# Attention projections with low parts of their weights from adding transfers, and the depthwise convolution moved forward, in a hybrid encoder layer

## The chip, the core and the metric

One core of a Trainium2 chip runs the whole program. The metric is the device time of one execution in microseconds (us). Five engines matter: TensorE (PE) for matrix products, VectorE (DVE), ScalarE (ACT) and GpSimd (POOL) for everything elementwise, and SyncE (SP), which issues most of the transfers from memory. Each engine works through its own instructions strictly in the order in which they stand in its queue, and waits by semaphores for what another engine or a transfer has to finish first.

## The reference

One layer on 512 tokens of width 1024, in fp32, with three sub-layers, each normalised first and added to the residual stream:

```
h = rms_norm(x);  p = h @ w_in          # q, k, v | conv input | ssm input
o_sb   = stick_breaking(rms_norm(q), rms_norm(k), v)   # 8 heads x 64
o_conv = conformer(p)   # GLU, causal depthwise conv of 31 taps on 256
                        # channels, LayerNorm, swish, 256x256 projection
o_ssm  = s5(p)
x = x + concat(rms_norm(o_sb), rms_norm(o_conv), rms_norm(o_ssm)) @ w_out
x = x + cross_attention(rms_norm(x), rms_norm(mem))    # 4 heads x 256
gate, up = rms_norm(x) @ ffn_w_in
x = x + (silu(gate) * up) @ ffn_w_out                  # hidden 2816
```

Stick-breaking attention needs, for each row of scores z, the log-sigmoid of -z under a causal mask, its running sum from the right, and an exponential.

## The kernel before

**Products in three parts.** PE works on fp32r operands, and a plain product would lose bits. So each operand x is held as a rounded high part and a low part, x minus the high part, and each product is three matmuls into one PSUM accumulator: high by high, high by low, low by high (`mm3`, L105 to L109). An activation is split by ACT, which casts, and DVE, which subtracts (`split`, L113/L114, or L116/L117 where a gain goes in).

**Weights.** `load_w` (L88 to L96) does the same for a piece of weights of up to 128x1024: SP loads it into a staging tile (tag `wst`, three buffers, L93), ACT casts it into `whi` (L94), and DVE subtracts into `wlo` (L95). `whi` and `wlo` have four buffers each (WB), and all weights of the program go through these rings. A staging buffer is free again when both the cast and the subtraction have read it. `gemm_rows` (L224) runs one product over the rows of K: it loads two K-slices at a time for all four row tiles, and keeps the last `tail` slices for a finish tile by tile, with their chunks loaded together ahead of it. For the attention projections the tail is TP, four slices, that is two chunks.

**What sets the order.** Outside one block, a scheduler orders the instructions of each engine by the order of the program text, shifted where `tc.high_priority(offset)` asks for it. The text itself mixes generators: `weave(main, side)` takes from `main` a number of nanoseconds and lets `side` issue products until their estimated time is used up; `along(main, side, n)` advances `side` by n steps for each step of `main`; `steps(x)` runs a generator out at once.

**The mixing stage** (span 0 to 308 us). First the input norm and the products of the SSM; beside the SSM's chain, as side work, the convolution's input products (`conv_gemm`), then the projections of q, k and v for the head pairs 0 and 1 (`sb_proj`, L663; tiles `ws00` to `ws16`). Then the attention chain (`sb_chain`): per head pair a front (`sb_front`, L675: norm of q and k on ACT and DVE, transposes, splits) and six groups of scores (`sb_weights`, L697: scores on PE, three passes on ACT, then on DVE the sum `sa` L720, the running sum `ss` L722 and a difference, an exponential on ACT), turned and multiplied with v two groups later (`sb_turn`, `sb_out`). Its side work is `sb_proj(2)` and `sb_proj(3)` (tiles `ws20` to `ws36`), then the output projection of the convolution and SSM branches (`mixed_out`), the memory's norm, keys and values.

**The convolution** is 60 DVE steps on 128x512 (`conv_taps`, L611, after two that begin a half, L609): one tap of 31 for one of two channel halves, into the accumulator `cac`. They run two to a step of the projections 0 to 3. Its end, `conv_tail` (L614: transposes, LayerNorm, swish, the small projection `wpw`), runs beside `mixed_out` of the SSM branch, in the attention chain.

**The start of the feed-forward stage** (some 460 to 500 us) is written out by hand for all engines (`manual_schedule`, from L1309). It overlaps the last rows of cross-attention's output projection (`wo_rows`), the norm and transposes of the four row tiles (`hf_*`), and the first units of gate and up weights. The feed-forward products use Winograd's form of Strassen's scheme, with seven products where a block product has eight, so sums and differences of activation blocks (`hf_diff`, `hf_sum`: t1f to t4f) and of weight blocks (`unit_raw` L1236/L1237, `unit_tsum` L1252/L1253) are formed first, and each is split. Of units 0 and 1, `unit_a` casts the two plain blocks on ACT (L1244) and subtracts on POOL (L1245, tiles `wa00`, `wa01`); the differences of `hf_sum` (L1223) are POOL's but for one, and so is the second sum of `unit_raw`.

## Time and profile before

| | |
|---|---|
| median of 3 runs (lowest to highest) | 834.74 us (833.09 to 836.9) |
| the profiled execution | 835.77 us, span 833.7 us |
| mean granted TensorE clock | 0.971 |
| PE busy | 786.9 us, 94% of the span |
| DVE busy | 653.8 us, 78% |
| ACT busy | 397.4 us, 48% |
| POOL busy | 187.9 us, 23% |
| mean DMA rate | 91 GB/s |

The span reaches from the first to the last instruction on the core; times of the trace count from its start. A row of a group names line, engine, operation, written and read tiles with their forms, the number of instructions, then busy us, the mean ns of one, and the idle time in front with what ended it. A row of the timeline begins with start and length in us. A row of the busy time by stretches gives for each engine its busy us and, in brackets, its instructions.

### The profile page before, as it was taken

How to read it: one execution, taken by the hardware profiler on the slowest of the kernel's cores; microseconds unless marked ns; L12 is line 12 of the kernel's file. 1: busy time of each engine (PE TensorE's matmuls, PEld its weight loads, DVE VectorE, ACT ScalarE, POOL GpSimd, SP SyncE). 2: the span in 40 equal slices, each digit the busy share in tenths (PEclk: the TensorE clock that was granted, in tenths of full speed). 3: DMA queues.
4: the chain of work that ended last, by engine and by line, in shares of the span. 5: the costliest groups of instructions: out<-in, count | busy, mean ns of one | idle time of the engine just before them, and what ended most of it. 6: DMA issues, size and time to landing. Idle time of an engine off the chain costs nothing.

```text
span 833.7 us, 12174 instructions
## 1 busy us (share of the span) xinstructions
PE 786.9 (94%) x4640; PEld 688.3 (83%) x4640; DVE 653.8 (78%) x1100; ACT 397.4 (48%) x729; POOL 187.9 (23%) x150
## 2 busy tenths in 40 slices
PE   5699999988899989999999869999999999999998
PEld 3678999876677768888888769999999999888886
DVE  8979989999889968566846898899999997333333
ACT  6334364767676846354634644444444443223221
POOL 4910000000000000000001456677666661000000
PEclk9989999989699999999999979999999999999999
DMA  5210223041312432420342022333333321322322
GB/s 217 70 58 26 77 76 97 17 152 53 125 64 67 137 98 91 137 77 26 119 139 72 26 76 88 115 103 102 102 103 127 115 88 51 101 83 95 101 76 101
DMA packets 22523, 76.07 MB, mean 91 GB/s; under 512 B 2753, under 2 KB 3009, under 8 KB 22466
## 3 DMA queue, kind: packets, MB, share of 16 engines
q1 hardware_dynamic: 22466, 75.31, 28.3%
q8 instruction: 36, 0.59, 0.3%
q14 instruction: 21, 0.17, 0.1%
HBM read 73.20 MB, written 2.10 MB: 90 GB/s over the span
## 4 chain that ended last, share of the span: by engine, by line
PE 72%; DVE 18%; ACT 5%; issue 2%; DMA 1%; POOL 0%; DVEq 0%; SPq 0%; POOLq 0%; ACTq 0%
PE fo L108 5%; PE fo L107 5%; PE fo L109 5%; PE f L108 2%; PE f L107 2%; PE f L109 2%; PE xo L107 2%; PE xo L109 2%; PE xo L108 2%; DVE cac L611 2%; PE xq L107 2%; PE xq L109 2%; PE xq L108 2%; DVE ss L722 1%; DVE hfbl L114 1%
## 5 line engine op out<-in xcount | busy, mean ns | idle before, releaser
L1237 POOL TENSOR_TENSOR wgb<-wga,wgb 128x512 f32<-128x512 f32 x22 | 43.4, 1971 | 138.1 <-DMA wga<-in_w_gu_dram 133.1
L760 POOL TENSOR_TENSOR sqa<-sqa,sq 128x512 f32<-128x512 f32 x3 | 3.8, 1283 | 259.1 <-ACT sq L759 259.1
L1236 POOL TENSOR_TENSOR wgb<-wgb 128x512 f32<-128x512 f32 x20 | 35.9, 1796 | 40.8 <-DMA wgb<-in_w_gu_dram 28.1
L611 DVE SCALAR_TENSOR_TENSOR cac<-hp,pk,cac 128x512 f32<-128x512 f32 x60 | 44.2, 757 | 0.0
L1301 POOL TENSOR_TENSOR aF<-aF,fup 128x1024 f32<-128x1024 f32 x10 | 34.7, 3468 | 5.5 <-DVE fup L1297 4.6
L1253 POOL TENSOR_TENSOR wga<-wga 128x512 f32<-128x512 f32 x20 | 25.9, 1295 | 23.9 <-DVE wga L1252 23.9
L1252 DVE TENSOR_TENSOR wga<-wgb,wga 128x512 f32<-128x512 f32 x22 | 23.1, 1051 | 0.2
L113 ACT CAST wTh<-wT 128x384 fp32r<-128x384 f32 (+2 forms) x40 | 14.5, 371 | 8.3 <-PE wT L736 6.7
L722 DVE TENSOR_TENSOR_SCAN ss<-ones,sa 128x512 f32<-128x512 f32 (+1 forms) x16 | 17.4, 1089 | 0.0
L114 DVE TENSOR_TENSOR wTl<-wT,wTh 128x384 fp32r<-128x384 f32 (+2 forms) x40 | 16.3, 420 | 1.5 <-ACT wTh L113 1.3
L717 ACT ACTIVATE sa<-z 128x384 f32<-128x384 f32 (+1 forms) x24 | 12.7, 527 | 9.6 <-PE z L712 9.5
L709 PE MATMUL z<-kh,qh 64*128 64x512 f32 (+3 forms) x32 | 13.6, 424 | 3.9 <-DVE ss L723 2.6
L709 PEld LDWEIGHTS z<-kh,qh 64*128 64x128 f32 x32 | 6.1, 189 | 12.4 <-issue 4.8
L736 PE MATMUL wT<-ident,ss 128*128 128x128 f32 x80 | 14.0, 297 | 2.1 <-DVE ql L117 2.1
L720 DVE SCALAR_TENSOR_TENSOR sa<-z,sa 128x384 f32<-128x384 f32 (+1 forms) x24 | 14.4, 601 | 1.8 <-ACT sa L719 1.7
L724 ACT ACTIVATE ss<-ss 128x384 f32<-128x384 f32 (+1 forms) x24 | 13.5, 561 | 3.2 <-DVE ss L723 3.1
L723 DVE TENSOR_TENSOR ss<-z,ss 128x384 f32<-128x384 f32 (+1 forms) x24 | 14.4, 601 | 0.0
L718 ACT ACTIVATE sa<-sa 128x384 f32<-128x384 f32 (+1 forms) x24 | 13.6, 566 | 0.3
L719 ACT ACTIVATE sa<-sa 128x384 f32<-128x384 f32 (+1 forms) x24 | 13.5, 562 | 0.4
L736 PEld LDWEIGHTS wT<-ident,ss 128*128 128x128 f32 x80 | 9.8, 151 | 4.1 <-DVE ql L117 2.3
L1299 ACT ACTIVATE aF<-aF 128x1024 f32<-128x1024 f32 x11 | 11.6, 1056 | 2.2 <-DVE aF L1297 2.2
L107 PE MATMUL o<-wTh,vzh 128*128 128x512 f32 (+3 forms) x32 | 11.5, 359 | 1.1 <-ACT wTh L113 1.1
(2188 smaller groups left out, 3271.2 us busy)
## 6 DMA issues: line engine op xcount, KB each, us to landing
wgb<-in_w_gu_dram SPq DMA_DIRECT2D x22, 512.0 KB, 3.3
wga<-in_w_gu_dram SPq DMA_DIRECT2D x22, 512.0 KB, 3.5
for<-in_w_fo_dram SPq DMA_DIRECT2D x22, 512.0 KB, 3.3
xr<-in_x_dram SPq DMA_DIRECT2D x4, 512.0 KB, 5.2
out_dram<-xr SPq DMA_DIRECT2D x8, 256.0 KB, 2.0
xbh<-in_x_dram SPq DMA_DIRECT2D x2, 512.0 KB, 4.9
xbl<-in_x_dram SPq DMA_DIRECT2D x2, 512.0 KB, 7.8
mt<-in_mem_dram SPq DMA_DIRECT2D x2, 512.0 KB, 4.4
```

The costliest lines, as they stand in the source:

```text
L107: te.matmul(o, a[0], b[0], start=start, stop=False)
L108: te.matmul(o, a[0], b[1], start=False, stop=False)
L109: te.matmul(o, a[1], b[0], start=False, stop=stop)
L114: v.tensor_tensor(lo, src, hi, op=ALU.subtract)
L611: v.scalar_tensor_tensor(a, x, w, a, op0=ALU.mult, op1=ALU.add)
L722: v.tensor_tensor_scan(ts[:, ::-1], d0, ta[:, ::-1], 0.0, op0=ALU.mult, op1=ALU.add)
L736: te.transpose(pt[:, b * P:(b + 1) * P], ts[:, b * P:(b + 1) * P], ident)
L1236: eng.tensor_tensor(b[:, 0], b[:, 1], b[:, 2], op=ALU.add)
L1237: g.tensor_tensor(b[:, 1], a[:, 0], b[:, 1], op=ALU.subtract)
L1252: v.tensor_tensor(a[:, 0], b[:, 0], a[:, 0], op=ALU.subtract)
L1253: eng.tensor_tensor(a[:, 1], a[:, 1], a[:, 0], op=ALU.subtract)
L1301: (g if i + 1 < len(units) else v).tensor_tensor(aF[p], aF[p], dst, op=ALU.mult)
```

## The change

Seven edits:

- The low part of the sixteen chunks of the attention projections is formed in another way. ACT casts as before, then writes the negated high part into the low tile; then a transfer, issued by POOL, reads the weights from memory a second time and adds them to that tile. DVE has no part in it. The order in which these loads are issued is shifted forward by 1200 (EV_QUEUE).
- TP is 2 instead of 4: the finish tile by tile holds one chunk instead of two.
- The taps run three to a step of the projections instead of two, and those that are left after `sb_proj(2)` run out before `sb_proj(3)`.
- The end of the convolution runs beside `sb_proj(3)` instead of beside `mixed_out` of the SSM branch.
- `hf_sum` is DVE's throughout.
- The plain blocks of units 0 and 1 (`unit_a`) get their low part by an adding transfer too, as above.
- In `unit_raw` of units 0 to 3 both sums are DVE's; before, DVE had the first sum of units 0 and 1.

```diff
--- before.py
+++ after.py
@@ -38,7 +38,7 @@
 C2 = math.floor((TWO_PI - C1) * 2.0 ** 21) / 2.0 ** 21
 C3 = TWO_PI - C1 - C2
 WB = 4
-TQ, TK, TP = 4, 2, 4
+TQ, TK, TP = 4, 2, 2
 DEPTH = 2
 FRONT = 2
 
@@ -52,6 +52,7 @@
            3500, 0, 2500, 2600, 4100, 3500)
 
 EV_CONV, EV_QKV, EV_OUT, EV_SB = 900, 800, 800, 1700
+EV_QUEUE = 1200
 
 PK = {}
 _o = 0
@@ -85,19 +86,25 @@
         n = {"acc": 4, "z": 2, "tp": 2}[tag]
         return pp.tile([P, 512], F32, tag=tag, bufs=n, name=name)
 
-    def load_w(src, n, name):
+    def load_w(src, n, name, queue=False):
+
 
         st = wp.tile([P, 1024], F32, tag="wst", bufs=3, name=name + "s")
         hi = wp.tile([P, 1024], F32R, tag="whi", bufs=WB, name=name + "h")
         lo = wp.tile([P, 1024], F32R, tag="wlo", bufs=WB, name=name + "l")
         nc.sync.dma_start(st[:, :n], src)
         s.copy(hi[:, :n], st[:, :n])
-        v.tensor_tensor(lo[:, :n], st[:, :n], hi[:, :n], op=ALU.subtract)
+        if queue:
+            s.activation(lo[:, :n], hi[:, :n], AF.Copy, scale=-1.0)
+            g.dma_start(lo[:, :n], src, accum_op=ALU.add)
+        else:
+            v.tensor_tensor(lo[:, :n], st[:, :n], hi[:, :n], op=ALU.subtract)
         return hi, lo
 
-    def load_k(w, k, n, name):
-
-        return load_w(w[:, k:k + 2, :].rearrange("p k n -> p (k n)"), 2 * n, name)
+    def load_k(w, k, n, name, queue=False):
+
+        with tc.high_priority(offset=EV_QUEUE if queue else 0):
+            return load_w(w[:, k:k + 2, :].rearrange("p k n -> p (k n)"), 2 * n, name, queue)
 
     def cols(parts, c):
         return [x[:, c] for x in parts]
@@ -221,7 +228,7 @@
         while late:
             late.pop(0)[1]()
 
-    def gemm_rows(acc, a, w, n, ks, name, k0, k1, tail=2):
+    def gemm_rows(acc, a, w, n, ks, name, k0, k1, tail=2, queue=False):
 
 
         def step(t, k, b, kk):
@@ -229,13 +236,13 @@
 
         head = len(ks) - tail
         for kc in range(0, head, 2):
-            b = load_k(w, ks[kc], n, f"{name}{kc}")
+            b = load_k(w, ks[kc], n, f"{name}{kc}", queue)
             for kk in range(2):
                 for t in range(len(acc)):
                     step(t, ks[kc + kk], b, kk)
                 tick()
                 yield 3 * len(acc) * n * 0.43
-        b = [load_k(w, ks[kc], n, f"{name}{kc}") for kc in range(head, len(ks), 2)]
+        b = [load_k(w, ks[kc], n, f"{name}{kc}", queue) for kc in range(head, len(ks), 2)]
         for t in range(len(acc)):
             for kc in range(tail):
                 step(t, ks[head + kc], b[kc // 2], kc % 2)
@@ -663,7 +670,7 @@
     def sb_proj(p):
         acc = [ps("acc", f"qkv{p}{t}") for t in range(NT)]
         yield from gemm_rows(acc, lambda k, t: [x[:, k, t * P:(t + 1) * P] for x in xn], A["w_sb"][p], 384, range(KD),
-                             f"ws{p}", 0, KD - 1, TP)
+                             f"ws{p}", 0, KD - 1, TP, queue=True)
         qk = raw.tile([P, NT, 256], F32, tag="qk", bufs=2, name=f"qk{p}")
         vz = vzs[p % 3]
         for t in range(NT):
@@ -996,13 +1003,13 @@
         v.tensor_scalar(gqs, pcol("gq"), 0.125, None, op0=ALU.mult)
 
         T = conv_taps()
-        side = chain(conv_gemm(), along(sb_proj(0), T, 2), along(sb_proj(1), T, 2))
+        side = chain(conv_gemm(), along(sb_proj(0), T, 3), along(sb_proj(1), T, 3))
         weave(S5, side)
         drain(side)
     mxs = [slotB("mxs" + i, F32R, i, 0) for i in "hl"]
     with tc.tile_pool(name="sbp", bufs=1, side="right") as sbp:
         CT = conv_tail()
-        side = chain(along(sb_proj(2), T, 2), along(sb_proj(3), T, 2), x_again(), *[along(mixed_out(mxc, 2, (6, 7), 4, hf), CT, 1) for hf in range(2)], steps(CT),
+        side = chain(along(sb_proj(2), T, 3), steps(T), along(sb_proj(3), CT, 1), steps(CT), x_again(), *[mixed_out(mxc, 2, (6, 7), 4, hf) for hf in range(2)],
                      mem_norm(), *[mixed_out(mxc, 1, (4, 5), 4, hf) for hf in range(2)], mem_turn(),
                      kv("xa_wk", 0), kv("xa_wk", 1), out_sb((0, 1, 2)))
         weave(sb_chain(sbp), side)
@@ -1216,7 +1223,7 @@
                 split(*at("22"), f1[:, :, c])
                 s.copy(f0[:, :, c], pts[t][0])
 
-        def hf_sum(nm, t, eng=g):
+        def hf_sum(nm, t, eng=v):
             c, _ = hf_cols(t)
             t1_, t2_, t3_, t4_ = [x[:, :, c] for x in (t1f, t2f, t3f, t4f)]
             o, a, b = {"T3": (t3_, t2_, t3_), "T2": (t2_, t2_, t1_), "T4": (t4_, b21[:, :, c], t2_)}[nm]
@@ -1234,7 +1241,7 @@
             nc.sync.dma_start(a.rearrange("p j n -> p (j n)"), A["w_gu"][p, x, 0])
             nc.sync.dma_start(b[:, 1:].rearrange("p j n -> p (j n)"), A["w_gu"][p, x, 1])
             eng.tensor_tensor(b[:, 0], b[:, 1], b[:, 2], op=ALU.add)
-            g.tensor_tensor(b[:, 1], a[:, 0], b[:, 1], op=ALU.subtract)
+            eng.tensor_tensor(b[:, 1], a[:, 0], b[:, 1], op=ALU.subtract)
             hb, lb = [ff.tile([P, 3, 512], F32R, tag="wb" + i, bufs=2, name=f"wb{p}{x}{i}") for i in "hl"]
             split(hb, lb, b)
             return a, b, {nm: (hb[:, i], lb[:, i]) for i, nm in enumerate(("S1", "S3", "22"))}
@@ -1247,6 +1254,14 @@
 
         def unit_a(p, x, a, b, w, eng=v):
             w["11"], w["12"] = unit_two(p, x, "a", a, eng)
+
+        def unit_a_queue(p, x, a, b, w):
+
+            h, l = [wp.tile([P, 2, 512], F32R, tag="w" + part, bufs=WB, name=f"wa{p}{x}{part}") for part in ("hi", "lo")]
+            s.copy(h, a)
+            s.activation(l, h, AF.Copy, scale=-1.0)
+            g.dma_start(l.rearrange("p j n -> p (j n)"), A["w_gu"][p, x, 0], accum_op=ALU.add)
+            w["11"], w["12"] = [(h[:, i], l[:, i]) for i in range(2)]
 
         def unit_tsum(p, x, a, b, w, eng=g):
             v.tensor_tensor(a[:, 0], b[:, 0], a[:, 0], op=ALU.subtract)
@@ -1304,7 +1319,7 @@
         ORD = (("tp", "22", "S2"), ("z", "S1", "S3"), ("acc", "S4"))
 
         def prep(i):
-            ws[i] = unit_raw(*units[i])
+            ws[i] = unit_raw(*units[i], v if i < 4 else g)
             unit_a(*units[i], *ws[i])
             unit_tsum(*units[i], *ws[i])
             unit_t(*units[i], *ws[i])
@@ -1318,14 +1333,14 @@
                 if t > 0:
                     hf_turn(t - 1)
                 if t == NT - 1:
-                    unit_a(*units[1], *ws[1], eng=g)
+                    unit_a_queue(*units[1], *ws[1])
                 wo_norm(t, acc)
                 if t == NT - 1:
                     hf_diff(t - 1)
                     unit_tsum(*units[0], *ws[0], v)
                 wo_scale(t)
                 if t == NT - 2:
-                    unit_a(*units[0], *ws[0], eng=g)
+                    unit_a_queue(*units[0], *ws[0])
                 if t > 0:
                     hf_split(t - 1)
             unit_start(0)
@@ -1340,7 +1355,7 @@
             hf_sum("T3", 3)
             hf_sum("T2", 3)
             unit_tsum(*units[1], *ws[1], v)
-            hf_sum("T4", 2, v)
+            hf_sum("T4", 2)
             hf_sum("T4", 3)
             for nm in ("T3", "T2", "T4"):
                 for t in (2, 3):
```

Where it moves instructions, three places. DVE's queue around the first group of attention weights (`sa_`, written by L720 before and by L727 after, on the scores `z_`), before: L117 and L114 are low parts of activations, L95 low parts of weights, `cac` is a tap.

```order
L117 SCALAR_TENSOR_TENSOR kl_1306<-kT_1300,pk,kh_1305 128x512
L611 SCALAR_TENSOR_TENSOR cac<-hp,pk,cac 128x512
L95 TENSOR_TENSOR ws24l<-ws24s,ws24h 128x768
L95 TENSOR_TENSOR ws26l<-ws26s,ws26h 128x768
L611 SCALAR_TENSOR_TENSOR cac<-hp,pk,cac 128x512
L95 TENSOR_TENSOR ws30l<-ws30s,ws30h 128x768
L611 SCALAR_TENSOR_TENSOR cac<-hp,pk,cac 128x512
L114 TENSOR_TENSOR vzl_98<-qkv_1309,vzh_97 128x2x64
L611 SCALAR_TENSOR_TENSOR cac<-hp,pk,cac 128x512
L95 TENSOR_TENSOR ws32l<-ws32s,ws32h 128x768
L611 SCALAR_TENSOR_TENSOR cac<-hp,pk,cac 128x512
L720 SCALAR_TENSOR_TENSOR sa_1412<-z_1407,sa_1412 128x512
```

After:

```order
L124 SCALAR_TENSOR_TENSOR ql_1333<-qT_1327,gqs,qh_1332 128x512
L618 SCALAR_TENSOR_TENSOR cac<-hp,pk,cac 128x512
L124 SCALAR_TENSOR_TENSOR kl_1342<-kT_1336,pk,kh_1341 128x512
L618 SCALAR_TENSOR_TENSOR cac<-hp,pk,cac 128x512
L101 TENSOR_TENSOR wpwl<-wpws,wpwh 128x512
L618 SCALAR_TENSOR_TENSOR cac<-hp,pk,cac 128x512
L121 TENSOR_TENSOR vzl_98<-qkv_1345,vzh_97 128x2x64
L727 SCALAR_TENSOR_TENSOR sa_1437<-z_1432,sa_1437 128x512
L121 TENSOR_TENSOR vzl_98<-qkv_1346,vzh_97 128x2x64
L729 SCALAR_TENSOR_TENSOR ss_1438<-ones_73,sa_1437 128x512
```

The low parts of `ws24` to `ws32` are gone from it. Taps stand in it still, but the last of them now comes ahead of the first group; before, taps followed it.

ACT's queue at the chunk `ws24`, in `sb_proj(2)`; `qk_` and `vzh_` are the copies that empty the accumulators of `sb_proj(1)`. Before:

```order
L94 CAST ws24h<-ws24s 128x768
L671 COPY qk_1252<-qkv_1115 128x256
L113 CAST vzh_95<-qkv_1115 128x2x64
L94 CAST ws26h<-ws26s 128x768
L94 CAST ws30h<-ws30s 128x768
```

After:

```order
L96 CAST ws24h<-ws24s 128x768
L678 COPY qk_1288<-qkv_1130 128x256
L98 ACTIVATE ws24l<-ws24h 128x768
L678 COPY qk_1288<-qkv_1131 128x256
L120 CAST vzh_95<-qkv_1130 128x2x64
L120 CAST vzh_95<-qkv_1131 128x2x64
```

The negated copy `ws24l` stands behind the cast, between two copies out of the accumulators; the transfer that adds to it is in POOL's queue.

DVE's queue at the start of the feed-forward stage, from the product that ends the norm of the last row tile; `hf.._` and `t1f` to `t4f` are activation blocks, `wga_` and `wgb_` weight blocks. Before:

```order
L1187 SCALAR_TENSOR_TENSOR hf_4608<-xr,rny,gbf 128x1024
L114 TENSOR_TENSOR hfT1l<-t1f,hfT1h 128x4x128
L114 TENSOR_TENSOR hfbl_4354<-t2f,hfbh_4352 128x4x128
L1203 TENSOR_TENSOR t1f<-nfp_4671,b_4360 128x4x128
L1245 TENSOR_TENSOR wt00lo<-wga_4390,wt00hi 128x1024
L114 TENSOR_TENSOR hfT1l<-t1f,hfT1h 128x4x128
L114 TENSOR_TENSOR hfbl_4354<-t2f,hfbh_4352 128x4x128
L1252 TENSOR_TENSOR wga_4400<-wgb_4401,wga_4400 128x512
L1253 TENSOR_TENSOR wga_4400<-wga_4400 128x512
L1223 TENSOR_TENSOR t4f<-b_4361,t2f 128x4x128
```

After:

```order
L1194 SCALAR_TENSOR_TENSOR hf_4626<-xr,rny,gbf 128x1024
L121 TENSOR_TENSOR hfT1l<-t1f,hfT1h 128x4x128
L121 TENSOR_TENSOR hfbl_4370<-t2f,hfbh_4368 128x4x128
L1230 TENSOR_TENSOR t3f<-t2f,t3f 128x4x128
L1243 TENSOR_TENSOR wgb_4896<-wgb_4896 128x512
L1230 TENSOR_TENSOR t2f<-t2f,t1f 128x4x128
L1210 TENSOR_TENSOR t1f<-nfp_4689,b_4376 128x4x128
L1252 TENSOR_TENSOR wt00lo<-wga_4406,wt00hi 128x1024
L121 TENSOR_TENSOR hfT1l<-t1f,hfT1h 128x4x128
L121 TENSOR_TENSOR hfbl_4370<-t2f,hfbh_4368 128x4x128
L1230 TENSOR_TENSOR t3f<-t2f,t3f 128x4x128
L1244 TENSOR_TENSOR wgb_4896<-wga_4895,wgb_4896 128x512
```

Among the splits (L114, now L121) stand the differences of `hf_sum` (L1230) and the sums of the later units' weights (L1243, L1244), which POOL had before.

## The prediction

> **What bounds the kernel now.** I read the page, then the busy time by stages, then the waits and the order of time inside the stages where TensorE (PE) is not full. The stages are my cut; columns are stretch, its length, then busy us of PE, PE's weight load, VectorE (DVE), ScalarE (ACT) and GpSimd (POOL), granted clock, DMA share, GB/s.
>
> ```profile
> PE 786.9 (94%) x4640; PEld 688.3 (83%) x4640; DVE 653.8 (78%) x1100; ACT 397.4 (48%) x729; POOL 187.9 (23%) x150
> ...
> 70.00:147.00 77.00, 74.88 (x428) 69.11 (x428) 73.84 (x132) 36.79 (x71) 0.00 (x0) 1.00 0.25 69
> 147.00:180.00 33.00, 31.34 (x174) 26.30 (x172) 33.00 (x61) 25.27 (x56) 0.00 (x0) 0.99 0.16 50
> 180.00:207.00 27.00, 25.02 (x117) 19.65 (x117) 24.42 (x55) 17.44 (x40) 0.00 (x0) 0.88 0.32 106
> 207.00:224.00 17.00, 12.96 (x33) 8.76 (x34) 15.36 (x25) 12.89 (x25) 0.00 (x0) 0.50 0.33 98
> 224.00:250.00 26.00, 24.73 (x131) 19.88 (x130) 21.77 (x50) 18.72 (x47) 1.29 (x1) 0.96 0.24 88
> 250.00:308.00 58.00, 55.35 (x283) 43.71 (x283) 48.02 (x95) 38.15 (x90) 2.56 (x2) 0.99 0.32 100
> 308.00:470.00 162.00, 161.58 (x816) 134.17 (x816) 110.32 (x225) 82.51 (x183) 7.09 (x4) 1.00 0.29 88
> 470.00:500.00 30.00, 19.70 (x127) 18.33 (x126) 29.72 (x34) 14.18 (x25) 17.29 (x10) 0.83 0.22 70
> 500.00:834.00 334.00, 328.58 (x2256) 304.62 (x2254) 237.78 (x280) 118.78 (x134) 128.38 (x66) 1.00 0.30 97
> ```
>
> The page's 94% for PE is an average over stages with two limits. From 308 to 470 and from 500 on PE is full (161.58 of 162, 328.58 of 334): time won before is kept there, and nothing is won inside. Two stretches are DVE's. From 147 to 180 it is busy 33.00 of 33, and over the attention chain (147 to 308) 142.6 of 161, the five rows added; PE, with each row's busy time times its clock, does 31.0 + 22.0 + 6.5 + 23.7 + 54.8 = 138 us of full-speed work there. From 470 to 500 DVE has 29.72 of 30, PE 19.70 at clock 0.83.
>
> **The attention stage.** The taps of the depthwise convolution (L611) and the low parts of weights (L95) stand in DVE's queue between the links of the chain.
>
> ```profile
> L611 DVE SCALAR_TENSOR_TENSOR cac<-hp,pk,cac 128x512 f32<-128x512 f32 x60 | 44.2, 757 | 0.0
> ...
> 70.00:147.00 77.00, 31.32 (x43) 1.00 0.25 69
> 147.00:308.00 161.00, 12.90 (x17) 0.92 0.27 89
> ...
> 119.72 1.42 DVE L611 SCALAR_TENSOR_TENSOR cac<-hp,pk,cac 128x512 f32<-128x512 f32 x2
> 121.04 0.69 DVE L681 TENSOR_REDUCE qss<-sq 128x8 f32<-128x512 f32 x1
> ...
> 135.54 0.75 DVE L117 SCALAR_TENSOR_TENSOR kl<-kT,pk,kh 128x512 fp32r<-128x512 f32 x1
> ...
> 137.73 0.96 DVE L95 TENSOR_TENSOR ws26l<-ws26s,ws26h 128x768 fp32r<-128x768 f32 x1
> 138.59 0.76 DVE L611 SCALAR_TENSOR_TENSOR cac<-hp,pk,cac 128x512 f32<-128x512 f32 x1
> ...
> 141.06 0.84 ACT L94 CAST ws32h<-ws32s 128x768 fp32r<-128x768 f32 x1 [0.43 <-DMA ws32s<-in_w_sb_dram]
> ...
> 143.75 0.69 DVE L720 SCALAR_TENSOR_TENSOR sa<-z,sa 128x512 f32<-128x512 f32 x1 [0.20 <-ACT sa L719]
> ...
> 169.06 0.87 DVE ws36l L95
> ```
>
> The two middle rows are the taps alone: 43 before 147, 17 after. Two in succession take 119.72 to 121.04, 0.66 each; a low part takes 137.73 to 138.59, 0.86. The first group of attention weights reaches DVE at 143.75.
>
> Per part. (a) Low parts: sixteen leave DVE, fourteen of them before the first group (12.0 us) and two (ws34, ws36) after it (1.7 us). (b) Taps: the order shows all sixty ahead of the first group; 17 (by the rows after 147) to 19 (counted from 143.75) move over it, 17 x 0.66 = 11.2 us. Ahead of the group DVE therefore loses 12.0 and gains 11.2: unchanged. Behind it DVE has 11.2 + 1.7 = 12.9 us less to do, in a stage where it sets the pace. The convolution's end is not made cheaper, only earlier: its products (the side work that PE takes between links) become free before 207 to 224, where PE now has 12.96 us at half clock. (c) What it takes: the first front (the norm of q and k) starts later in DVE's queue, and less work stands between its links. Its own links from qss at 121.04 to the group are about 12.5 us (two reductions 1.3, logarithm and exponential 0.5, four small steps behind a tap each 3, product 1.2, transposes 1, splits 2, scores 1.2, three ACT passes 1.9), and the new queue holds 12.3 us of DVE work there, so I put 1 to 2.5 us of waiting on it. I take 10.5 us for the stage. Bounds: 0 if idle time grows by all that was freed; 17 if DVE's freed time counts whole and 4 of the 10.5 us that PE lacks in 207 to 224 come on top. PE's 138 of 161 would allow 23.
>
> (d) ACT gets sixteen negated copies of 128x768. The nearest row is the cast of that shape, 0.84: 13.4 us, before 147 nearly all, where ACT has 36.79 of 77. What hides them is that idle time; without it they would cost their 13.4. They stand in front of the copies that empty PSUM (the order shows ws24's between them): each can hold these by 0.84 once, behind sums that PE does not need back at once (four accumulators).
>
> (e) The adding transfer itself, T from issue to landing, is not in this trace.
>
> ```profile
> wga<-in_w_gu_dram SPq DMA_DIRECT2D x22, 512.0 KB, 3.5
> ...
> SPq L93 <- DVE ws24l L95: 10.3, 1, 10.3
> ...
> 130.00:140.00 10.00, 10.00 (x62) 9.53 (x60) 10.00 (x15) 2.10 (x4) 0.00 (x0) 1.00 0.11 25
> ```
>
> Below, T is a plain load, 3.5 us for 512 KB. Above, three passes over the bytes (source, old destination, result), 10.5, an estimate from that row. I take 5, since one issue moves the same bytes out of memory. Cover: with four pairs of buffers and one-chunk tails, three chunks of 24 products lie between a buffer's release and its use; at 62 products in 10 us that is 3 x 3.9 = 11.6 us where PE is densest. Cast, copy and ACT's queue take up to 3, so T up to about 8.6 costs nothing; at 10.5 a ring of four takes 3.9 + 10.5 + 3 = 17.4 instead of 15.6, 0.45 a chunk, 3.6 us over the eight dense chunks. POOL's queue behind these issues holds only the three sums of squares (L760), the first of which comes after all sixteen. Staging buffers also come free on the cast: SP waited 10.3 us for DVE's ws24l, and the ws32s behind it held the first group's ACT work until 141.06.
>
> A page speaks against this part. The Trainium skill, SBUF — State Buffer, section "Who interferes with whom", says that transfers issued from GpSimd are starved of descriptors while VectorE runs instructions that take both port pairs, single-source copies and tensor_scalar above all. By that rule a transfer would wait at most one such instruction, because the taps and sums here have two inputs; no run here shows it yet, and the sum would stay as it is.
>
> **The start of the feed-forward stage.**
>
> ```profile
> 460.01 1.29 DVE L114 TENSOR_TENSOR hfa<-b,hfa 128x512 fp32r<-128x512 f32 x2
> ...
> 467.06 4.97 DVE L114 TENSOR_TENSOR hfa<-b,hfa 128x512 fp32r<-128x512 f32 x2 [0.64 <-ACT hfa L113]
> 471.96 0.68 DVE L1179 TENSOR_TENSOR xr<-xo,xr 128x512 f32<-128x512 f32 x1
> ...
> 475.37 1.28 DVE L1187 SCALAR_TENSOR_TENSOR hf<-xr,rny,gbf 128x1024 f32<-128x1024 f32 x1
> 476.57 1.76 DVE L114 TENSOR_TENSOR hfT1l<-t1f,hfT1h 128x512 fp32r<-128x512 f32 x1
> 478.26 1.77 DVE L114 TENSOR_TENSOR hfbl<-t2f,hfbh 128x512 fp32r<-128x512 f32 x1
> 479.95 0.68 DVE L1203 TENSOR_TENSOR t1f<-nfp,b 128x512 f32<-128x512 f32 x1
> ...
> 495.55 1.21 DVE L1245 TENSOR_TENSOR wt01lo<-wga,wt01hi 128x1024 fp32r<-128x1024 f32 x1
> ...
> 465.49 3.20 POOL L1245 TENSOR_TENSOR wa00lo<-wga,wa00hi 128x1024 fp32r<-128x1024 f32 x1 [18.32 <-ACT wa00hi L1244]
> 468.66 2.83 POOL L1245 TENSOR_TENSOR wa01lo<-wga,wa01hi 128x1024 fp32r<-128x1024 f32 x1
> 475.42 2.37 POOL L1223 TENSOR_TENSOR t3f<-t2f,t3f 128x512 f32<-128x512 f32 x1 [3.93 <-ACT t3f L1210]
> ...
> 467.46 1.04 ACT L1244 CAST wa01hi<-wga 128x1024 fp32r<-128x1024 f32 x1
> ```
>
> Two splits take 1.29 alone and 4.97 beside POOL's low parts: 3.7 lost. Others go from 0.64 to 1.76 beside POOL's differences. All that POOL work leaves. In steps: the pair of splits ends near 469.3, after one more ACT copy (1.04) ahead of it, and the last row's sum starts 2.65 earlier. ACT has the second copy (1.04) before that row's squares, so the row's norm ends at about 474.4, 2.3 before 476.65. Then two splits and three moved sums at 0.61 (3.05) put t1f at 477.4 (479.95 before). From t1f to the last split of t4f DVE took 15.6; now it is 1.2 for the t-part and 17 instructions at about 0.6, 11.3. End 488.7 against 495.6: 6.9 won. Against it: PE reaches the last row's transposes only after both unit starts, at 470.4 + T + 1.3, and t1f wants them by 477. T up to 5.2 costs nothing, and each us beyond costs one. Units 2 and 3 put four more sums on DVE; two lie in the 11.3, two (1.2 us) behind 500. I take 5.5; bounds 0 (T 10.5) and 7.5.
>
> **Sum.** 10.5 + 5.5 = 16 off the profiled execution, 835.77 (span 833.7): 819.8. The median shown, 834.74, lies 1.0 under that execution, so **819**. What changes by under 0.5% (830.6 to 838.9) this kernel's measurement cannot tell from none.
>
> **The rivals.** (1) Also PE's hole closes: the early convolution end feeds PE through 207 to 224, the clock stays up, 17 + 6 us: 812. For it: 33 products in 17 us there; against: ACT and DVE links still pace the groups. (2) The chain, not DVE's load, sets the pace once the taps are gone: 3 us in the attention stage, 5 in the other: 827. For it: 0.20 us of waiting for ACT already at 143.75; against: DVE full for 33 us on end. (3) The taps come too early: the first front starts 10.4 us later in DVE's queue (its place by summed durations, 112.9 against 123.3), and if its 22.7 us from 121.04 to 143.75 stay whole, the attention stage wins nothing: 829 to 831. Against: 17 taps and low parts stood inside those 22.7. (4) Slower: the adding transfers are long, and PE waits for low parts. At T 13 a ring takes 3.9 + 13 + 3 = 19.9, 1.1 more a chunk, 8.6 over eight; the other stage loses 7.8 of its 5.5: the gain is gone. From there each us costs 3; at T 15, 6 us slower, 841. For it: nothing in the trace bounds T; against: it needs nearly four times a plain load.
>
> **How the numbers follow.** Forecast 0.50, (1) 0.16, (2) 0.19, (3) 0.09, (4) 0.06. Faster: 0.50 + 0.16 + 0.19 and a third of (3), 0.88; same 0.07 (the rest of (3), and part of T near 13); slower 0.05. Range 811 to 830, which leaves (4), most of (3) and the far side of (1) out.
>
> **What would show it.** Right: first group at 143 to 147, all taps before it; end of the attention chain near 298 instead of 309.6; no half clock around 207 to 224; splits at 0.6 to 0.7 and t4f's last split near 489. Wrong: PE waiting for DMA ws..l, adding transfers above 9 us, or DVE idle in the chain by 12 us more than 18.

## The result and the profile after

The changed kernel takes 825.41 us (median of 4 runs, 824.38 to 826.56), 0.9878 of the time before (interval 0.9839 to 0.9917). By the medians, 834.79 and 825.41, it is 9.4 us faster, by the ratio 10.2; 15.7 were forecast. The ratio is not the quotient of the two medians, and in the experiments it differs from it by up to 0.0027. The time lies inside the forecast range, which was 19 us wide, and nearest to the time of rival (2). The profiled execution took 826.56, span 824.5, granted clock 0.972.

Of the forecast's two gains the second came out in size and the first came to less than half. The end of the attention chain (the first row that adds the attention branch to the residual, 309.60 before) moved by 3.9 us, and the time from there to the end of the span went from 524.1 to 824.5 - 305.68 = 518.8, by 5.3. In the order of time on DVE, after (L688 was L681, L727 was L720, L1024 was L1017):

```profile
133.00 0.68 DVE L688 TENSOR_REDUCE qss<-sq 128x8 f32<-128x512 f32 x1
...
148.11 0.69 DVE L727 SCALAR_TENSOR_TENSOR sa<-z,sa 128x512 f32<-128x512 f32 x1 [0.24 <-ACT sa L726]
...
305.68 2.73 DVE L1024 SCALAR_TENSOR_TENSOR xr<-wos,rb,xr 128x512 f32<-128x512 f32 x4
```

The first group comes 4.4 us later than before (143.75), as all sixty taps are ahead of it, and the front begins 12.0 later (133.00 against 121.04). The busy time by stretches of the kernel after (stretch, length, PE, its weight load, DVE, ACT, POOL, clock, DMA share, GB/s):

```profile
147.00:180.00 33.00, 32.62 (x187) 27.99 (x185) 26.74 (x60) 29.16 (x67) 1.72 (x2) 1.00 0.42 98
180.00:207.00 27.00, 21.77 (x74) 15.82 (x74) 19.64 (x43) 20.12 (x50) 0.00 (x0) 0.62 0.53 175
207.00:224.00 17.00, 16.99 (x87) 12.91 (x86) 16.52 (x35) 10.65 (x25) 0.00 (x0) 1.00 0.11 27
224.00:250.00 26.00, 26.00 (x133) 20.56 (x132) 25.01 (x40) 16.47 (x34) 1.70 (x1) 1.00 0.24 75
250.00:300.00 50.00, 48.72 (x249) 37.77 (x248) 44.00 (x91) 37.66 (x91) 1.56 (x1) 1.00 0.29 88
```

DVE is no longer full from 147 to 180: 26.74 of 33, where it had 33.00. But PE has a hole (a stretch in which it idles and its clock falls) from 180 to 207, 21.77 of 27 at clock 0.62. Behind it, from 207 to 250, PE is full, 42.99 of 43, and DVE nearly so, 41.53. The hole that stood at 207 to 224 before has not gone; a like one now stands earlier. What PE waits for in it:

```profile
180.50 0.50 PE L114 MATMUL pw<-cvh,wpwh 128*128 128x512 f32 x1 [0.46 <-ACT cvh L120]
...
183.36 0.44 PE L716 MATMUL z<-kh,qh 64*128 64x384 f32 x1 [1.31 <-DVE ss L730]
...
187.17 1.22 PE L114 MATMUL pw<-cvh,wpwh 128*128 128x512 f32 x2 [1.48 <-ACT cvh L120]
...
188.99 0.80 PE L115 MATMUL pw<-cvl,wpwh 128*128 128x512 f32 x1 [0.60 <-DVE cvl L121]
...
193.80 0.59 PE L283 MATMUL bss<-ones,csq 128*128 128x1 f32 x2 [1.07 <-ACT csq L666]
```

Four of these are the convolution's own products (pw) and its sum of squares (csq). They stand in PE's queue ahead of every product of mixed_out, the first of which starts at 206.58, and wait for the swish and its split on ACT and DVE: with one more wait of 0.32, 3.9 of the 5.2 us in which PE idles. The fifth, z, waits 1.31 for a running sum of the attention chain. No single gap is longer than 1.48 us, yet the clock falls to a half: in stretches of 5 us it is 0.94 from 180, and 0.50 or 0.51 from 185 to 205. In the hole of the kernel before the longest waits were the chain's, for the split of the next front and for a running sum; the next dense product, of mixed_out's convolution branch, came only behind the last pw:

```profile
208.61 1.75 PE L736 MATMUL wT<-ident,ss 128*128 128x128 f32 x7 [2.09 <-DVE ql L117]
...
216.76 0.79 PE L709 MATMUL z<-kh,qh 64*128 64x512 f32 x1 [1.36 <-DVE ss L723]
...
222.68 0.80 PE L107 MATMUL wo<-wo010h,mxch 128*128 128x512 f32 x1
```

The start of the feed-forward stage, PE first, then DVE:

```profile
465.36 0.28 PE L115 MATMUL f<-hfa,wa00hi 128*128 128x256 f32 x1
468.47 0.58 PE L116 MATMUL f<-hfa,wa00lo 128*128 128x256 f32 x1 [2.83 <-DMA wa00lo<-in_w_gu_dram]
...
474.33 0.46 PE L116 MATMUL f<-hfa,wa01lo 128*128 128x256 f32 x1 [0.37 <-DMA wa01lo<-in_w_gu_dram]
...
475.70 1.03 PE L1201 MATMUL nfp<-ident,hf 128*128 128x128 f32 x8
```

```profile
464.32 1.29 DVE L121 TENSOR_TENSOR hfa<-b,hfa 128x512 fp32r<-128x512 f32 x2 [1.72 <-ACT hfa L120]
...
476.33 0.69 DVE L1210 TENSOR_TENSOR t1f<-nfp,b 128x512 f32<-128x512 f32 x1 [2.93 <-PE nfp L1201]
...
486.03 1.28 DVE L121 TENSOR_TENSOR hfbl<-t4f,hfbh 128x512 fp32r<-128x512 f32 x2
```

The pair of splits takes 1.29 instead of 4.97. But PE waits 2.83 us for the first adding transfer, and DVE 2.93 for the transposes that PE comes to late. The transfers themselves, from issue to landing (last column, us):

```profile
wa00lo<-in_w_gu_dram POOLq DMA_DIRECT2D x1, 512.0 KB, 5.5
wa01lo<-in_w_gu_dram POOLq DMA_DIRECT2D x1, 512.0 KB, 7.1
...
ws10l<-in_w_sb_dram POOLq DMA_DIRECT2D x1, 384.0 KB, 5.0
...
ws32l<-in_w_sb_dram POOLq DMA_DIRECT2D x1, 384.0 KB, 6.3
```

### The profile page after: what moved, and what is told of

Its sections match the earlier page's. It is cut to its first block, busy times and chain, and to the rows that moved or that the text cites. A ratio compares the mean times of both kernels' runs of the same rounds, so it can differ in the third digit from the quotient of the medians.

```text
span 824.5 us, 12231 instructions
## 1 busy us (share of the span) xinstructions
PE 787.4 (95%) x4640; PEld 687.9 (83%) x4640; DVE 631.3 (77%) x1095; ACT 408.4 (50%) x747; POOL 180.4 (22%) x155
## 4 chain that ended last, share of the span: by engine, by line
PE 81%; DVE 10%; ACT 3%; issue 2%; DMA 1%; POOL 0%; DVEq 0%; POOLq 0%; ACTq 0%
PE fo L115 5%; PE fo L114 5%; PE fo L116 5%; PE f L116 2%; PE f L114 2%; PE f L115 2%; PE xo L114 2%; PE xo L115 2%; PE xo L116 2%; PE qkv L114 2%; PE qkv L115 2%; PE qkv L116 2%; PE xq L114 2%; PE xq L116 2%; PE xq L115 2%
## 5 line engine op out<-in xcount | busy, mean ns | idle before, releaser
L618 DVE SCALAR_TENSOR_TENSOR cac<-hp,pk,cac 128x512 f32<-128x512 f32 x60 | 42.3, 743 | 0.0
L1243 POOL TENSOR_TENSOR wgb<-wgb 128x512 f32<-128x512 f32 x18 | 32.9, 1827 | 40.5 <-DMA wgb<-in_w_gu_dram 30.3
L1268 POOL TENSOR_TENSOR wga<-wga 128x512 f32<-128x512 f32 x20 | 28.8, 1440 | 41.3 <-DVE wga L1267 41.3
L1244 POOL TENSOR_TENSOR wgb<-wga,wgb 128x512 f32<-128x512 f32 x18 | 34.5, 1919 | 0.3
L121 DVE TENSOR_TENSOR wTl<-wT,wTh 128x384 fp32r<-128x384 f32 (+2 forms) x40 | 16.2, 415 | 1.4 <-ACT wTh L120 1.3
L727 DVE SCALAR_TENSOR_TENSOR sa<-z,sa 128x384 f32<-128x384 f32 (+1 forms) x24 | 14.3, 596 | 2.4 <-ACT sa L726 2.4
L726 ACT ACTIVATE sa<-sa 128x384 f32<-128x384 f32 (+1 forms) x24 | 13.5, 564 | 0.3
L803 DVE SCALAR_TENSOR_TENSOR xr<-wo,rb,xr 128x512 f32<-128x512 f32 x16 | 11.8, 742 | 0.3 <-PE wo L116 0.3
```

Of the source, the lines that this page charges most:

```text
L121: v.tensor_tensor(lo, src, hi, op=ALU.subtract)
L618: v.scalar_tensor_tensor(a, x, w, a, op0=ALU.mult, op1=ALU.add)
L1243: eng.tensor_tensor(b[:, 0], b[:, 1], b[:, 2], op=ALU.add)
L1244: eng.tensor_tensor(b[:, 1], a[:, 0], b[:, 1], op=ALU.subtract)
L1268: eng.tensor_tensor(a[:, 1], a[:, 1], a[:, 0], op=ALU.subtract)
```

## The experiments

Two theories came out of these rows. The **load theory** is the prediction's: DVE's work sets the pace of the attention stage. The **hole theory**: PE sets the end of the stage, by what it loses while it waits in order for the convolution's end with no dense product (a long run of matmuls that waits for nothing) in between. All times of a kernel are given as a ratio to the kernel before on the same chip; 0.01 is 8.3 us. Beside them stand two lengths from the profiled execution, free of how it started: **c - s**, from ACT's cast of the first projection chunk (ws00) to the end of the attention chain, and **end - c**, from there to the end of the span. Each kernel has one profile, so these two come from one execution each.

| kernel | ratio (interval) | c - s | end - c |
|---|---|---|---|
| before | 1 | 255.7 | 524.1 |
| the change | 0.9878 (0.9839 to 0.9917) | 251.1 | 518.8 |
| e1, attention part only | 0.9947 (0.9920 to 0.9974) | 252.1 | 523.2 |
| e2, feed-forward part only | 0.9969 (0.9940 to 0.9998) | 257.8 | 519.5 |
| e3, low parts on DVE | 1.0049 (1.0020 to 1.0077) | 265.1 | 519.0 |
| e4, convolution where it was | 0.9936 (0.9906 to 0.9965) | 254.4 | 519.1 |
| e5, end spread | 0.9806 (0.9779 to 0.9832) | 247.0 | 520.2 |
| e6, end late | 0.9911 (0.9884 to 0.9939) | 255.9 | 519.3 |
| e7, unit low parts on DVE | 0.9859 (0.9832 to 0.9886) | 252.3 | 515.1 |
| e8, sums on POOL | 0.9920 (0.9896 to 0.9944) | 252.8 | 522.9 |
| e9, e5 and e7 together | 0.9772 (0.9734 to 0.9811) | 247.6 | 514.7 |
| e10, unit low parts on POOL | 0.9888 (0.9843 to 0.9932) | 252.1 | 517.2 |
| e11, without the shift | 0.9959 (0.9935 to 0.9984) | 255.7 | 519.1 |
| e12, end spread, low parts on DVE | 0.9936 (0.9912 to 0.9961) | 256.9 | 520.6 |

Kernels with the same mixing stage show how far c - s can be trusted: 255.7 and 257.8 with that of before (before, e2), 251.1 to 252.8 with that of the change (the change, e1, e7, e8, e10). The medians of these groups differ by 4.6 us. In the same way end - c is 518.8 to 520.6 with the feed-forward code of the change (the change, e2 to e6, e11, e12), median 519.2, and 524.1 and 523.2 with that of before (before, e1): 4.4 us. The sum, 9.0, is close to the 9.4 of the times.

### The two parts apart

e1 leaves the feed-forward part out, e2 keeps it alone:

```diff
 e1
-                    unit_a_queue(*units[1], *ws[1])
+                    unit_a(*units[1], *ws[1], eng=g)
 ...
-        def hf_sum(nm, t, eng=v):
+        def hf_sum(nm, t, eng=g):
 ...
-            eng.tensor_tensor(b[:, 1], a[:, 0], b[:, 1], op=ALU.subtract)
+            g.tensor_tensor(b[:, 1], a[:, 0], b[:, 1], op=ALU.subtract)
 e2
-TQ, TK, TP = 4, 2, 2
+TQ, TK, TP = 4, 2, 4
 ...
-                             f"ws{p}", 0, KD - 1, TP, queue=True)
+                             f"ws{p}", 0, KD - 1, TP)
 ...
-        side = chain(conv_gemm(), along(sb_proj(0), T, 3), along(sb_proj(1), T, 3))
+        side = chain(conv_gemm(), along(sb_proj(0), T, 2), along(sb_proj(1), T, 2))
 ...
```

> Only the attention part of the change; the start of the feed-forward stage is as before (low parts of units 0 and 1, hf_sum and the second weight sums back on POOL). Theory A (the two parts are separate, as the trace after reads: the end of the attention chain moved from 309.6 to 305.7): 3.9 us faster than before, 831. Rival B (the parts are not separate: the attention part's early end helps the other stage, or the other way): under 2 or over 6 us faster.

> Only the feed-forward part of the change; mixing stage as before. Theory A (the parts are separate): 9.4 - 3.9 = 5.5 us faster than before, 829.3. Rival B: under 3.5 or over 7.5 us faster.

e1 gained 4.4 us (1 - 0.9947), e2 2.6 (interval 0.2 to 5.0). e2 lies below theory A's 5.5, and in its rival's bounds, by the times; its profile has the part's gain, end - c 519.5 against 524.1, and lost 2.1 of it in a mixing stage whose code is the same as before. Sum 7.0 against 10.2 for the change: within the intervals, the parts are separate, and each is worth some 4 to 5 us.

### Is it DVE's load?

e3 gives the low parts back to DVE and keeps the rest; e4 keeps the transfers and puts the convolution back:

```diff
 e3
-                             f"ws{p}", 0, KD - 1, TP, queue=True)
+                             f"ws{p}", 0, KD - 1, TP)
 e4
-        side = chain(conv_gemm(), along(sb_proj(0), T, 3), along(sb_proj(1), T, 3))
+        side = chain(conv_gemm(), along(sb_proj(0), T, 2), along(sb_proj(1), T, 2))
 ...
-        side = chain(along(sb_proj(2), T, 3), steps(T), along(sb_proj(3), CT, 1), steps(CT), x_again(), *[mixed_out(mxc, 2, (6, 7), 4, hf) for hf in range(2)],
+        side = chain(along(sb_proj(2), T, 2), along(sb_proj(3), T, 2), x_again(), *[along(mixed_out(mxc, 2, (6, 7), 4, hf), CT, 1) for hf in range(2)], steps(CT),
```

> The change, but the low parts of the sixteen attention projection chunks are subtracted on DVE again (no negated copy, no adding transfer, no shift of their order); taps, convolution end, TP 2 and the feed-forward part as changed. Load theory (DVE's load sets the pace of the attention stage): 13.7 us of work come back to DVE, 14 x 0.86 = 12.0 of it ahead of the first group, which then comes at about 158 to 160; the kernel is 11 to 14 us slower than the change, 836 to 839. Hole theory (PE sets the end of the stage from 205 on, because it stands behind the convolution's end from 180 to 205 and then works off a backlog): the groups move later, but the hole shrinks as the end of the convolution is spread over a longer chain; 2 to 6 us slower than the change, 827 to 831.

> The change, but the convolution's taps run two to a step again and its end runs beside mixed_out of the SSM branch, as before; adding transfers, TP 2 and feed-forward part as changed. Load theory: 17 taps (11 us) come back behind the first group and leave the stretch ahead of it: the first group at 138 to 141, and the end of the chain as in the change, since the sum of DVE's work is the same: 824 to 827. Hole theory: the hole of PE stays as long as before (17 us at half clock, some 12 us lost) but later, with less DVE work around it: 822 to 826, with half clock again at some 200 to 225. Rival (the tap move itself carries the gain): 830 to 834.

e3 is slower than the kernel before, and 14 us slower than the change: the load theory's number. Most of it goes in the stretch ahead of the first group, the change first, then e3:

```profile
70.00:147.00 77.00, 75.08 (x428) 68.70 (x427) 72.54 (x132) 43.17 (x76) 10.32 (x12) 1.00 0.65 131
```

```profile
70.00:147.00 77.00, 64.09 (x343) 59.49 (x342) 73.79 (x128) 28.85 (x54) 0.00 (x0) 0.91 0.19 52
```

With three taps to a step in front of the low parts, PE starves: 64.09 of 77 at clock 0.91. The first group comes 105.2 us after the cast of ws00, 93.5 in the change; the 11.7 between them match the fourteen low parts of 0.86 (12.0). e3 also lacks the forward shift of the loads, but that does not make this stretch: e11 below, which lacks the shift alone, has PE busy 75.27 of 77 at clock 1.00 there, and its first group 93.4 after the cast. So the taps can only be moved if the low parts leave DVE. e4 is the other half of that: the transfers alone free DVE of as much, and c - s falls by 1.3 to 3.4 us only (254.4). The load theory said 824 to 827 for it, the hole theory 822 to 826, the rival, by which moving the taps carries the gain, 830 to 834. It came to 829.4 (0.9936 of 834.74, interval 826.9 to 831.8; by the medians, 827.70 and 835.28, the ratio would be 0.991), so its time decides between none of the three. None saw that in e4, with DVE free, the last tap starts at 146.29 even at two to a step. Its stretches:

```profile
180.00:207.00 27.00, 24.78 (x129) 18.83 (x128) 25.96 (x60) 21.44 (x49) 0.00 (x0) 0.96 0.31 112
207.00:224.00 17.00, 14.34 (x38) 9.08 (x38) 12.85 (x17) 11.82 (x22) 0.00 (x0) 0.57 0.27 93
224.00:250.00 26.00, 24.14 (x125) 19.32 (x124) 21.97 (x53) 15.99 (x41) 1.97 (x1) 0.92 0.14 51
250.00:300.00 50.00, 49.09 (x231) 37.82 (x231) 42.58 (x85) 36.31 (x86) 1.64 (x1) 0.94 0.35 106
```

PE's hole stands where it stood before. From the first group to the end of the attention chain DVE has 137.4 us of work, 9.4 less than the 146.8 before, and that length is 165.1 us, 0.8 less than the 165.9 before. Ahead of the first group DVE's load counts; behind it, taking work from DVE alone brought next to nothing.

### Is it PE's hole?

e5 spreads the eight steps of the convolution's end over eighteen steps of products, so that dense products stand between them in PE's queue. e6 puts the end back beside mixed_out alone, with the taps early:

```diff
 e5
+    def every(x, k):
+        for _ in x:
+            yield 0
+            for _ in range(k - 1):
+                yield 0
 ...
-        side = chain(along(sb_proj(2), T, 3), steps(T), along(sb_proj(3), CT, 1), steps(CT), x_again(), *[mixed_out(mxc, 2, (6, 7), 4, hf) for hf in range(2)],
+        slow = every(CT, 2)
+        side = chain(along(sb_proj(2), T, 3), steps(T), along(chain(sb_proj(3), x_again(), *[mixed_out(mxc, 2, (6, 7), 4, hf) for hf in range(2)]), slow, 1), steps(slow),
 e6
-        side = chain(along(sb_proj(2), T, 3), steps(T), along(sb_proj(3), CT, 1), steps(CT), x_again(), *[mixed_out(mxc, 2, (6, 7), 4, hf) for hf in range(2)],
+        side = chain(along(sb_proj(2), T, 3), steps(T), sb_proj(3), x_again(), *[along(mixed_out(mxc, 2, (6, 7), 4, hf), CT, 1) for hf in range(2)], steps(CT),
```

> The change, but the steps of the convolution's end are spread over sb_proj(3) and both halves of mixed_out of the SSM branch, one step to two of theirs, so that dense products stand between them in PE's queue. Hole theory (PE waits in order for the convolution's end from 180 to 205, loses 5.2 us idle and 10.3 us to the half clock): the hole closes by a half or more, 4 to 10 us faster than the change, 815 to 821. Rival (ACT and DVE links set the pace there whatever PE does): the clock stays up, but the end comes at the same time: within 2 us of the change, 823.5 to 827.5.

> The change, but the convolution's end runs beside mixed_out of the SSM branch as before; the taps stay early. Hole theory: eight steps stand again between eight pieces of product that last some 4 us in all, so the hole only moves to about 200 to 225: within 4 us of the change, 822 to 829. Load theory (where the end stands is indifferent to DVE's load): within 2 us of the change.

e5 is 6.0 us faster than the change (0.9806 against 0.9878), as the hole theory had it; the end of the chain comes at 297.75. Of the profiled executions e5's also reaches the cast of ws00 3.9 us earlier (50.75 against 54.63), which no edit of e5 explains; c - s leaves that out, and is 247.0 in e5 and 247.6 in e9, which has the same mixing stage, where the five kernels with that of the change have 251.1 to 252.8. e6 is 2.8 slower than the change, inside the hole theory's 4 and past the load theory's 2 by less than the intervals; its c - s of 255.9 leaves nothing of the stage's gain. The stretches of e5:

```profile
180.00:207.00 27.00, 26.66 (x138) 21.48 (x137) 24.77 (x48) 20.14 (x44) 0.00 (x0) 1.00 0.49 162
207.00:224.00 17.00, 14.60 (x70) 10.58 (x69) 15.98 (x35) 14.47 (x35) 0.00 (x0) 0.99 0.21 67
224.00:250.00 26.00, 24.52 (x107) 18.91 (x106) 23.81 (x40) 15.45 (x31) 1.70 (x1) 0.81 0.30 89
250.00:300.00 50.00, 48.65 (x253) 37.63 (x254) 41.17 (x91) 34.91 (x88) 2.71 (x2) 1.00 0.29 89
```

The first hole is closed, and a smaller one has opened at 224 to 250. Put into one number: what PE loses from 180 to 300 is 120 less the sum of busy time times clock over the four stretches. With the low parts off DVE:

| kernel | PE lost, 180 to 300 | c - s | c - s less the loss |
|---|---|---|---|
| the change | 14.8 | 251.1 | 236.3 |
| e4 | 19.7 | 254.4 | 234.7 |
| e5 | 10.4 | 247.0 | 236.6 |
| e6 | 18.6 | 255.9 | 237.3 |
| e9 | 11.3 | 247.6 | 236.3 |
| e11 | 19.6 | 255.7 | 236.1 |

c - s differs by 8.9 us among these six, c - s less the loss by 2.6. The kernel before fits too: 20.1 lost (47.67 of full-speed work in its last 50), 235.6. So do e1, e2, e7, e8 and e10 (236.3 to 238.5); e3 and e12 do not, as they lose most ahead of 147. What each gained in the attention stage is what PE lost less. This is bookkeeping: it says where the time went. That the order in the queues makes the loss is shown by e5, which only moves the steps of the convolution's end within it.

DVE's work does not follow the length in the same way. From the first group to the end of the chain:

| kernel | DVE's work | length |
|---|---|---|
| before | 146.8 | 165.9 |
| the change | 133.4 | 157.6 |
| e5 | 133.5 | 151.5 |
| e6 | 134.1 | 160.4 |
| e11 | 135.0 | 162.3 |

The last four differ by 1.6 us in work and by 10.8 in length.

e12 is e5 with the low parts on DVE (the diff of e3 on that of e5):

> The change with the convolution's end spread as in the run with the spread end, but the low parts of the sixteen projection chunks subtracted on DVE again. Load theory (the low parts on DVE, with the taps three to a step, starve PE before the first group: PE 64 of 77 us busy in 70 to 147 in the run with DVE's low parts): 9 to 13 us slower than the spread end with transfers, 829 to 833. Hole theory alone (with the hole closed, PE makes up for it): within 5 us of it, 820 to 825.

It is 10.9 us slower than e5 (0.9936 against 0.9806), and like e3 it lacks the shift too: closing the hole does not make up for a PE that starves before 147 (63.65 busy of 77, clock 0.91).

### The start of the feed-forward stage

Three kernels take one of its edits back or another way: e7 subtracts the low parts of units 0 and 1 on DVE, e10 on POOL as before, e8 puts the sums back on POOL and keeps the transfers.

```diff
 e7
-                    unit_a_queue(*units[1], *ws[1])
+                    unit_a(*units[1], *ws[1])
 ...
-                    unit_a_queue(*units[0], *ws[0])
+                    unit_a(*units[0], *ws[0])
 e10
-                    unit_a_queue(*units[1], *ws[1])
+                    unit_a(*units[1], *ws[1], eng=g)
 ...
 e8
-        def hf_sum(nm, t, eng=v):
+        def hf_sum(nm, t, eng=g):
 ...
-            ws[i] = unit_raw(*units[i], v if i < 4 else g)
+            ws[i] = unit_raw(*units[i])
```

> The change, but the low parts of units 0 and 1 (wa00, wa01) are subtracted on DVE, without adding transfer or negated copy. Theory W (PE's wait for the two transfers, 2.83 + 0.37 us, and the half clock from 468.5 to 474.3 behind it, set when the last row's transposes come): the low part is there at about 463, PE reaches the transposes at about 471 instead of 475.7, DVE closes its gap of 2.93: 2 to 4.5 us faster than the change, 821 to 823.5. Rival (DVE is the bound of that stretch: 2.4 us more work for it): within 1 us or slower by up to 2.4, 824.5 to 828.

> The change, but the low parts of units 0 and 1 are subtracted on POOL as before (two instructions of some 3 us, beside DVE's splits); hf_sum and the weight sums stay on DVE. Theory K (the splits lengthened by POOL cost as much as the wait for the adding transfers): from the end of the attention chain to the end within 1.2 us of the change's 518.8, so 824 to 826.5. Rival L (the contention is the dearer one, as the prediction has it, 3.7 us): 3 to 5 us slower, 828 to 830.

> The change, but hf_sum (all but one) and the second weight sums of the first units are back on POOL; low parts of units 0 and 1 by adding transfers. Theory P (POOL's work beside DVE's splits lengthens both, the splits to 1.76 as in the profile before, and the differences take POOL 2.4 each): 3 to 6 us slower than the change, 828.5 to 831.5. Rival (only the low parts of the weights on POOL cost DVE time, the differences have slack): within 1.5 us of the change.

By end - c the code of the change has 519.2 (the median above), e8 522.9, e10 517.2, e7 and e9 515.1 and 514.7. So the sums on DVE bring 3.7 us of the 4.4, and the adding transfers bring nothing here: POOL's subtractions, which they took away, do no worse (2.0 better, little outside the scatter of 1.8), and DVE's 4.3 better. The times alone do not tell e7 from the change (0.9859 against 0.9878, 1.6 us, where theory W had 2 to 4.5), nor e10; e9 against e5 gives 2.8 (0.9772 against 0.9806), inside the intervals. DVE's rows of e10, then of e7:

```profile
463.70 4.97 DVE L121 TENSOR_TENSOR hfa<-b,hfa 128x512 fp32r<-128x512 f32 x2 [0.64 <-ACT hfa L120]
...
476.21 0.68 DVE L1210 TENSOR_TENSOR t1f<-nfp,b 128x512 f32<-128x512 f32 x1
```

```profile
464.71 1.29 DVE L121 TENSOR_TENSOR hfa<-b,hfa 128x512 fp32r<-128x512 f32 x2
465.92 1.22 DVE L1252 TENSOR_TENSOR wa01lo<-wga,wa01hi 128x1024 fp32r<-128x1024 f32 x1
...
474.69 0.68 DVE L1210 TENSOR_TENSOR t1f<-nfp,b 128x512 f32<-128x512 f32 x1
```

In e10 the pair of splits takes its 4.97 again, and t1f still starts at 476.21, no later than in the change (476.33): from 465 to 480 DVE runs without a gap of note, while in the change it waits 2.93 us for PE. What the contention with POOL cost, the wait for the transfer costs now. In e7 neither is there, at 2.4 us of DVE's time, and t1f starts 2.7 us earlier than in the change, counted from the end of the attention chain. The sums are another matter; DVE in the change, then DVE in e8, then POOL in e8:

```profile
470.31 0.69 DVE L121 TENSOR_TENSOR hfT1l<-t1f,hfT1h 128x512 fp32r<-128x512 f32 x1
```

```profile
468.28 1.78 DVE L121 TENSOR_TENSOR hfT1l<-t1f,hfT1h 128x512 fp32r<-128x512 f32 x1
...
477.32 1.78 DVE L1267 TENSOR_TENSOR wga<-wgb,wga 128x512 f32<-128x512 f32 x1
```

```profile
467.45 2.06 POOL L1230 TENSOR_TENSOR t3f<-t2f,t3f 128x512 f32<-128x512 f32 x1 [1.48 <-ACT t3f L1217]
```

Beside POOL's differences DVE's instructions take 1.78 for 0.69. t1f comes as far behind the end of the attention chain in e8 as in the change (170.65 us), and from there on DVE has no gap to take it from: the last split of t4f ends 2.9 us later.

### The shift, and the best of both

e11 sets EV_QUEUE to 0. e9 joins e5 and e7.

```diff
-EV_QUEUE = 1200
+EV_QUEUE = 0
```

> The change without the forward shift of the sixteen projection loads (EV_QUEUE 0 instead of 1200). Theory (the adding transfers, 5.0 to 6.3 us from issue to landing, are covered by the ring of four buffers; PE waited for none of them): within 1.5 us of the change, 824 to 827. Rival (the shift is what covers them): PE waits for some of ws14 to ws20, whose negated copies ACT now has later, by 1 us each: 3 to 5 us slower, 828 to 830.

> The change with both edits of the earlier runs: the convolution's end spread over sb_proj(3) and both halves of mixed_out of the SSM branch, and the low parts of units 0 and 1 subtracted on DVE. The two lie in different stages. Theory (they add): the spread end brought the end of the attention chain from 305.7 to 297.8, the DVE low parts made the time from there to the end 3.7 shorter (518.8 to 515.1): 8 to 11 us faster than the change, 814.5 to 817.5. Rival (what is won ahead is lost at the start of the feed-forward stage, by loads that then come late): 5 to 7 us faster, 818 to 820.5.

e11 missed both expectations: 6.8 us slower than the change (0.9959 against 0.9878), though no product of the projections waits for an adding transfer, in its trace or in the change's. Its rows from 240 on show a second half-clock stretch that the change does not have:

```profile
240.00:245.00 5.00, 2.88 (x11) 2.02 (x11) 5.00 (x14) 4.59 (x12) 0.00 (x0) 0.84 0.00 0
245.00:250.00 5.00, 5.00 (x13) 3.32 (x13) 4.14 (x7) 0.68 (x2) 0.00 (x0) 0.50 0.00 0
250.00:260.00 10.00, 10.00 (x46) 7.94 (x45) 6.36 (x10) 6.95 (x13) 0.00 (x0) 0.82 0.17 51
```

PE waits there 1.56 us for a running sum of the chain and 1.24 for the low part of the memory's tile (hm). Its loss of 19.6 and c - s of 255.7 put 3.6 to 4.6 us down to that hole. The rest is not in the trace: its profiled execution was the shortest of twelve (827.47; the others 830.59 to 832.73). It also reached the cast of ws00 3.7 us earlier than the change's, and with as late a start it would have come to 831.2, among the others; that they started late is not shown. Why a shift of loads that have all landed by some 170 changes what PE meets at 240 stays open.

e9 came out as forecast: 816.25 us, 0.9772, some 19 us under the kernel before and 8.8 under the change, faster than both. TP of 2 is the one edit of the mixing stage that no run takes back by itself.

## Why the prediction was right, and where it was not

The time fell inside the range and the right way. The forecast of 819 was 6.4 us too low, and the wide range had room for it; the reason given for the larger gain did not hold.

- **The first group** (143 to 147, all taps ahead of it). It came at 148.11, 1.1 us past that bound, with the front 12.0 later (10.4 forecast) and 15.1 from the front to the group (12.5 of links and 1 to 2.5 of waiting forecast). All taps were ahead of it. Counted from the cast of ws00, the group came 3.7 later than before. The price of the low parts ahead of the group, 12.0, was measured by e3 as 11.7.
- **"Behind it DVE has 12.9 us less to do, in a stage where it sets the pace": 10.5 us.** This is the step that failed. The stage gained 3.9 by the two profiles, 4.6 between the groups of equal code, and its end came at 305.68 where "near 298" was the mark. DVE did get lighter behind the first group, by 13.5 us (146.82 to 133.35), but 5.2 of it became idle time of DVE and the length fell by 8.3; less the 3.7 by which the group came later, that is 4.6. DVE full for 33 us on end was not what set the end of the stage; the time that PE loses was. e4 lightens DVE and gains 1.3 to 3.4; e5 leaves DVE's work as it is and gains 4 more.
- **"The convolution's end is not made cheaper, only earlier: its products become free before 207 to 224."** The rows of that stretch were read as a PE short of products, and it was: between the chain's links and the convolution's end no dense product stood. What the reading left out is that the end's own products wait for ACT and DVE in PE's queue. Moved forward and run out at once, the end made a hole where it now stood: 5.2 us idle and 8.3 by the clock (21.77 x 0.38) at 180 to 207, where 207 to 224 had 4.0 and 6.5.
- **The mark "no half clock around 207 to 224"** held, and was too narrow: it was met by a half clock at 185 to 205.
- **T, the adding transfer, 5 us taken, 3.5 to 10.5 as bounds.** Measured 5.0 to 6.3 for 384 KB and 5.5 and 7.1 for 512 KB. In the attention stage no product waits for one, as forecast up to 8.6. Rival (4) falls with it.
- **The feed-forward stage, 5.5 us.** 5.3 came by the two profiles, 4.4 between the groups of equal code, but not by the steps named, so that the size is in part luck. The pair of splits gave its 3.7 on DVE (1.29 for 4.97), but that gain did not reach the end: the first transfer held PE 2.83 us, PE then worked at half clock up to 474.3, and t1f came 3.9 + 476.33 - 479.95 = 0.3 later than before, by the stage's own clock, where 2.5 earlier was forecast. From t1f to the last split, 11.0 us (476.33 to 487.31) against 11.3 forecast and 15.6 before: the sums' step was right, and it alone carries the gain. The price "each us beyond 5.2 costs one" makes 1.9 of the second transfer's 7.1; 2.8 were lost, with PE at half clock in between, which the price left out.
- **The rivals.** (1), the hole closes, is what the kernel could have had: e5 and e9 reach it in part, with 10.4 and 11.3 still lost. (2) has the time, 827, and the 5 of the feed-forward stage, but its chain was not what stood in the way. (3), the attention stage wins nothing, has the later front right and its end wrong.

## What to carry to other kernels

An engine that is full on end need not be the one that sets the end: sum up what TensorE loses, idle time and clock together, over the stage, and ask what each wait in its queue is ordered behind. A serial piece of work with a few products in it (a norm, an activation, a small projection) cost TensorE much of its latency here wherever it was run out in one go; spread its steps among dense products before moving it. Work that is taken from a full engine pays where the links of the chain stand behind it, and moving other work into the place pays only with it: here either half alone brought 1.3 to 3.4 us of the attention stage (e4) or cost 7.3 to 9.4 (e3).
